# The written key of each head pair turned through DRAM and VectorE's blocks, and the outputs' transposes moved behind the joined visit

## The chip, the cores and the metric

One core of a Trainium2 chip runs the kernel in one launch. The engines are TensorE (PE: matmuls and transposes; its weight loads are listed apart as PEld), VectorE (DVE), ScalarE (ACT), GpSimd (POOL) and SyncE (SP); SP and ACT also issue the DMAs, each in its own order. The metric is device time in microseconds, the median of several runs of the same program.

## The reference

One layer of a hybrid decoder over 512 positions and 2,048 channels, in fp32, then a final RMSNorm. What matters here is the first half of the channels: 16 heads of 64 channels with a gated delta-rule recurrence.

```
z = rms_norm(x) @ W_in           # r, k, v, two small inputs, gate | pool input, pool gate
w = exp(-exp(-softplus(-(w0 + tanh(wd) @ Wup)) - 0.5));  a = sigmoid(a0 + ad @ Aup)
kk = normalised(k * k_k);  k = k * (1 + (a - 1) * k_a)
S_t = S_{t-1} * w_t - (S_{t-1} kk_t)(kk_t a_t)^T + v_t k_t^T;   y_t = S_t r_t
y = group_norm(y) + (r . k . r_k) v;  times silu(gate)
pool branch: trailing means over 2/4/8/16 positions, a map per group, times silu(gate)
x = x + concat(y, pool) @ W_out;  x = x + sigmoid(x @ W_pg + b) * (p @ W_ple)
```

## The kernel before

Every large product is made of three matmuls of split operands (a high part and a rest), on tiles of 128 channels by 512 positions. The input is normalised and transposed once (`hhi`, `hlo`). The recurrence then runs in eight rounds of two heads (j = 0 to 7, 128 channels each), in chunks of 64 positions (8 a round). Within a round the chunk-by-chunk state update is a chain of small matmuls with short DVE and ACT steps between them. Between these the kernel issues pieces of a long stream of large matmuls (`pump(n)` issues n of them): the projections of the next rounds and of the pool branch (tiles zk, zr, zv, zg, zb). In this part PE's instructions keep the order of the program; the other engines' orders are set by a scheduler with priorities. Behind the rounds come the projection with W_out (acc_o) and the gate's with W_pg (acc_g).

The weights come by `wsplit`: SP issues the load of 256 KB into `raw` (four buffers), ACT makes the high part (L132, four buffers), DVE the rest (L133). SP's queue goes in order, and a load waits there until its buffer is free.

The steps of a round, as the change touches them:

- `prepare(j)` (DVE, L591 to L601, then a split) makes the written key `bk`: for each chunk, 128 columns with the two products that are written into the state (line 596 one half, line 600 the other), with channels on partitions.
- `scores(j)` multiplies `bk` by the read side `ar` (matmuls pm), masks the result into `mt` and sends a part of it to DRAM (`nd`, four writes) and back (`n`, two reads into 32x32 systems). It runs inside the previous round's `recur`, behind that round's first chunk.
- `invert(j)`: 31 short DVE steps (tm, xw) that invert the 32x32 triangles, two steps at each hand-over of the previous round's recurrence; the result goes through DRAM (`xd`) to `x1`.
- `gather(j)`: transposes v (pv) and the written key (pbk) on PE, with ACT copies out of PSUM: `bkn` is the key with positions on partitions. Here stand also the next round's decay and key norms, and the previous round's output (`pending.pop()()`, below). Then the joined visit: y1 = block transposes of x1 on DVE (L723), matmuls pq, pmv, px, and copies on ACT that complete x1 (L745).
- `recur(j)`: per chunk py and the add zs on DVE (the first hand-over of the chunk), pu and its copy uv on ACT, ps (with `bkn`) and the state's update sbd on DVE. Behind the eighth chunk come the outputs' statistics and their normalisation (`ysb`, L842 to L851).
- `finish`, kept in `pending` by `recur(j-1)` and called in `gather(j)`: transposes `ysb` (pyt, 4 transposes), scales it on ACT (yo), two products on DVE (L861, L862), and a store to DRAM that ACT issues (L863).

Of the kernel before, what the change touches and what calls it, by code (L numbers as in the profile page):

```python
# [9 lines left out]
F32 = mybir.dt.float32  # L10
# [3 lines left out]
ALU = mybir.AluOpType  # L14

P = 128
T = 512
# [4 lines left out]
NJ = DR // P  # L22
LORA = 64
C = 64
NCH = T // C
# [9 lines left out]
def trunk_kernel(ctx: ExitStack, tc: tile.TileContext, x, p, norm_g, w_in, mu, w0, w_up, a0, a_up,  # L35
                 k_k, k_a, r_k, ln_w, ln_b, w_pool, pool_scale, w_out, w_ple, w_pg, b_pg, final_g, out):
    nc = tc.nc
# [122 lines left out]
    def tr(*a):  # L160
        i = nc.tensor.transpose(*a)
        return tc.keep_in_program_order(i) if pin[0] else i
# [414 lines left out]
    def prepare(j):  # L577
        k_, r_, v_ = need("k", j), need("r", j), need("v", j)
        pw, ipw, tha = pws.pop(j)
        kk = kks.pop(j)  # L580
        if j + 1 < NJ:
            load_ab(j + 1)


        ar = rw.tile([P, NCH // 2, 4, C], F32, name=f"ar{j}", tag="ar", bufs=2)
        bk = rw.tile([P, NCH // 2, 4, C], F32, name=f"bk{j}", tag="bk")
        k4 = kk.rearrange("p (q c t) -> p q c t", c=2, t=C)
        pw4 = pw.rearrange("p (q c) t -> p q c t", c=2)
# [11 lines left out]
        nc.vector.tensor_tensor(bk[:, :, 1:3, :], k4, i4, ALU.mult)  # L600
        nc.vector.scalar_tensor_tensor(kp, r_, dp(49, j), kp, ALU.mult, ALU.mult)  # L601
        kph = rw.tile([P, T], F32R, name=f"kph{j}", tag="t", bufs=4)
        kpl = rw.tile([P, T], F32R, name=f"kpl{j}", tag="t", bufs=4)
        split(kph, kpl, kp)

        st_[j] = dict(pw=pw, ar=ar, bk=bk, v_=v_, kp=(kph, kpl))

    def scores(j):
        ar, bk, v_ = (st_[j][n_] for n_ in ("ar", "bk", "v_"))
        kph, kpl = st_[j].pop("kp")  # L610

        mt = rw.tile([P, 2, 8, 2, C], F32, name=f"mt{j}", tag="mt", bufs=2)
# [13 lines left out]


        ps = psM.tile([P, T], F32, name=f"pbo{j}", tag="m")
        mm(ps, blk, kph, start=True, stop=False)
        mm(ps, blk, kpl, start=False, stop=True)  # L630
        bv = rw.tile([P, T], F32, name=f"bv{j}", tag="bv", bufs=2)
        nc.vector.tensor_tensor(bv, ps, v_, ALU.mult)

        nd = dram.tile([2, 2, 8, 32, 32], F32, name=f"nd{j}", tag="nd")
        for par in range(2):
            pb = 64 * (1 - par)
            for b in range(2):
                rows = slice(pb + 32 * b, pb + 32 * b + 32)
                nc.sync.dma_start(out=nd[par, b].rearrange("u r c -> r u c"),
                                  in_=mt[rows, par, :, 1 - par, 32 * b:32 * b + 32])  # L640
        nb = []
        for i in range(2):
            t_ = rw.tile([P, 16, 32], F32, name=f"n32{j}_{i}", tag=("kk", "kp")[i])
            nc.sync.dma_start(out=t_, in_=nd[:, :, :, 16 * i:16 * i + 16, :].rearrange(
                "a b u r c -> (a b u) r c").unsqueeze(0).to_broadcast([4, 32, 16, 32]))
            nb.append(t_)
        st_[j].update(mt=mt, nb=nb, bv=bv)


    def invert(j):  # L650
# [26 lines left out]

    def gather(j):
        d = st_[j]
        bk, v_, mt = d.pop("bk"), d.pop("v_"), d["mt"]  # L680
        if j + 1 < NJ:
            prepare_key(j + 1)
            decay_and_rate(j + 1)
# [7 lines left out]
        nc.scalar.copy(uv[64:128, 1::2, :], pv[64:128])  # L691


        bkn = rw.tile([P, NCH, P], F32, name=f"bkn{j}", tag="bkn")
        for hf in range(2):
            ps = psM.tile([P, T], F32, name=f"pbk{j}_{hf}", tag="m")
            for i in range(4):
                ch = 4 * hf + i
                tr(ps[:, i * P:(i + 1) * P], bk[:, ch // 2, 2 * (ch % 2):2 * (ch % 2) + 2, :], ident)
            nc.scalar.copy(bkn[:, 4 * hf:4 * hf + 4, :], ps.rearrange("p (c n) -> p c n", n=P))  # L700

        pump(H4)

        d.update(uv=uv, bkn=bkn)
        if j + 1 < NJ:
            norm_key(j + 1)
        pump(H5)
        if pending:
            pending.pop()()
        pump(HX)  # L710

        x1 = d["x1"]
# [6 lines left out]
        y1 = rw.tile([P, 8, 32], F32, name=f"y1{j}", tag="tm")  # L719

        with tc.issue_after(late[0].ins):
            for pb in (0, 64):
                yt = nc.vector.transpose(y1[pb:pb + 32], x1[pb:pb + 32, :, 0:32])  # L723
# [23 lines left out]
        nc.scalar.copy(zsp[0][64:128, :].rearrange("p (h t) -> p h t", h=2), psv[64:128, 0:2, :])  # L747
        nc.scalar.copy(mv.rearrange("p q (h t) -> p (q h) t", h=2), psv)
        d["mv"] = mv
        pump(2 * H1)  # L750


    def recur(j, work, between):
        d = st_.pop(j)
        pw, ar, mt, bv, uv, bkn, mv, x1 = (d[n_] for n_ in ("pw", "ar", "mt", "bv", "uv", "bkn", "mv", "x1"))
        hop = [0]
        HC1, HC2, HC3 = HC
        lead = [None]
# [12 lines left out]
        for ch in range(NCH):  # L771
# [8 lines left out]
            if ch > 0:  # L780
# [67 lines left out]
        nt8 = rw.tile([P, 8, 1], F32, name=f"nt8{j}", tag="nt8")  # L848
        rsqrt(rs8, ve8, nt8)
        for i in range(8):  # L850
            nc.vector.tensor_scalar(y8[:, i, :], y8[:, i, :], mvr[:, i, 0:1], rs8[:, i, :],  # L851
                                    ALU.subtract, ALU.mult)

        def finish():
            sg = need("g", j)
# [11 lines left out]
    HC, HT, HX = (6, 9, 9), 130, 13  # L867
    HS, HN = 5, 2
    HP = 1000
    pending = []  # L870
    need("k", 0)
    need("r", 0)
    prepare_key(0)
# [304 lines left out]
```

## Time and profile before

| | us |
|---|---|
| median of 3 runs (1093.36 to 1094.28) | 1093.37 |
| the profiled execution | 1094.06 |
| its span, first to last instruction | 1092.3 |
| PE busy | 1067.4 |
| DVE busy | 707.9 |
| ACT busy | 448.2 |
| POOL busy | 74.4 |
| ACT copies out of pbk, 16 | 8.8 |

The granted TensorE clock is 0.998 of full. The rounds lie between about 110 and 727 us of the span, one about every 75 us. Rows of the timeline read: start, length, engine, line, operation, written tile <- read tiles, shape, count, and in brackets how long the engine had idled before it and what ended that. A matmul's length there is its latency: matmuls overlap, and the time that one takes of PE is the distance between starts. Rows of groups end with the busy time, the mean of one in ns, and the idle time before them. Rows of windows give, for a stretch, the busy time (and count) of PE, PEld, DVE, ACT and POOL, then the granted clock, the DMA engines' busy share and GB/s.

### The profile page before, as it was taken

Reading aid. Unit: us, or ns where it says so; the run is one execution under the profiler, and the core shown is the slowest. Engines: PE = TensorE matmul, PEld = TensorE weight load, DVE = VectorE, ACT = ScalarE, POOL = GpSimd, SP = SyncE. Lnnn points to the kernel's source line nnn. Section 1 sums busy time; section 2 is a strip of 40 time slices with the busy share of each in tenths; the row PEclk is TensorE's granted clock in tenths of the full one; section 3 lists DMA queues with packets and bytes.
Section 4 is the critical chain, followed back from the end, with each engine's and each line's share of the span. In section 5 each row is a group of like instructions: output and inputs, shape, how many; then the busy total and the mean of one; then the engine's idle time right before and its main releaser. Section 6 shows DMA issues by size and latency. Waiting matters only on the chain.

```text
span 1092.3 us, 17194 instructions
## 1 busy us (share of the span) xinstructions
PE 1067.4 (98%) x6060; PEld 879.1 (80%) x6060; DVE 707.9 (65%) x1835; ACT 448.2 (41%) x917; POOL 74.4 (7%) x180
## 2 busy tenths in 40 slices
PE   5999999999999999999999999999999999999996
PEld 4888878888888888787888788888888888888885
DVE  6687867878779679678886956454433424445366
ACT  7633534435335335353443344544222222233337
POOL 2100010110110110100101101000000000000000
PEclk9999999999999999999999999999999999999999
DMA  7433433332423333333334242774534438454534
GB/s 233 116 97 97 112 92 79 102 101 72 127 81 102 105 91 89 95 83 90 94 93 120 79 138 94 231 242 163 171 123 141 164 97 261 129 187 147 174 105 154
DMA packets 178485, 138.56 MB, mean 127 GB/s; under 512 B 34677, under 2 KB 139742, under 8 KB 178398
## 3 DMA queue, kind: packets, MB, share of 16 engines
q1 hardware_dynamic: 157694, 103.89, 32.2%
q10 hardware_dynamic: 20704, 33.56, 9.5%
q8 instruction: 48, 0.79, 0.3%
q14 instruction: 39, 0.32, 0.1%
HBM read 118.02 MB, written 18.87 MB: 125 GB/s over the span
## 4 chain that ended last, share of the span: by engine, by line
PE 88%; DVE 5%; DMA 3%; ACT 2%; issue 1%; SPq 0%; ACTq 0%; DVEq 0%
PE acc_o L157 16%; PE acc_g L157 16%; PE zb L157 15%; PE zv L157 8%; PE zr L157 7%; PE zg L157 7%; PE zk L157 6%; DMA n<-nd 2%; PE py L157 2%; PE pple L157 2%; PE pu L157 2%; PE pm L157 1%; PE pp L157 1%; PE ps L157 1%; PE pmv L157 1%
## 5 line engine op out<-in xcount | busy, mean ns | idle before, releaser
L133 DVE TENSOR_TENSOR wlo_g<-raw_g,whi_g 128x512 fp32r<-128x512 f32 x84 | 56.9, 683 | 78.7 <-ACT whi_g L132 78.5
L157 PE MATMUL zb<-hhi,whi_b 128*128 128x512 f32 x256 | 106.3, 415 | 0.0
L133 DVE TENSOR_TENSOR wlo_o<-raw_o,whi_o 128x512 fp32r<-128x512 f32 x64 | 43.9, 690 | 92.3 <-ACT whi_o L132 92.2
L157 PE MATMUL zb<-hhi,wlo_b 128*128 128x512 f32 x256 | 100.5, 393 | 0.0
L157 PE MATMUL acc_o<-whi_o,ylo 128*128 128x512 f32 x256 | 100.2, 391 | 0.0
L157 PE MATMUL acc_o<-whi_o,yhi 128*128 128x512 f32 x256 | 99.9, 390 | 0.0
L157 PE MATMUL zb<-hlo,whi_b 128*128 128x512 f32 x256 | 99.8, 390 | 0.0
L157 PE MATMUL acc_o<-wlo_o,yhi 128*128 128x512 f32 x256 | 99.7, 389 | 0.0
L132 ACT CAST whi_g<-raw_g 128x512 fp32r<-128x512 f32 x84 | 51.9, 620 | 105.5 <-PE acc_g L157 60.3
L157 PE MATMUL acc_g<-whi_g,x2hi 128*128 128x512 f32 x208 | 81.2, 391 | 0.0
L157 PE MATMUL acc_g<-wlo_g,x2hi 128*128 128x512 f32 x208 | 81.0, 389 | 0.0
L157 PE MATMUL acc_g<-whi_g,x2lo 128*128 128x512 f32 x208 | 80.6, 389 | 0.0
L132 ACT CAST whi_o<-raw_o 128x512 fp32r<-128x512 f32 x64 | 39.9, 623 | 97.8 <-PE acc_o L157 97.8
L813 POOL TENSOR_SCALAR s0p<-sbd,pw 64x64 f32<-64x64 f32 x96 | 56.7, 590 | 338.5 <-DVE sbd L806 253.7
L132 ACT CAST whi_b<-raw_b 128x512 fp32r<-128x512 f32 x64 | 39.7, 620 | 87.1 <-PE zv L157 34.9
L133 DVE TENSOR_TENSOR wlo_b<-raw_b,whi_b 128x512 fp32r<-128x512 f32 x64 | 43.7, 684 | 34.2 <-ACT whi_b L132 33.0
L157 PEld LDWEIGHTS zb<-hhi,wlo_b 128*128 128x128 f32 x256 | 48.0, 188 | 11.0
L661 DVE TENSOR_TENSOR xw<-xw,tm 128x60 f32<-128x60 f32 (+24 forms) x248 | 51.9, 209 | 6.8
L157 PEld LDWEIGHTS acc_o<-wlo_o,yhi 128*128 128x128 f32 x256 | 48.1, 188 | 10.0
L157 PEld LDWEIGHTS acc_o<-whi_o,ylo 128*128 128x128 f32 x256 | 48.1, 188 | 9.9
L157 PEld LDWEIGHTS acc_o<-whi_o,yhi 128*128 128x128 f32 x256 | 48.1, 188 | 9.6
L157 PEld LDWEIGHTS zb<-hhi,whi_b 128*128 128x128 f32 x256 | 48.3, 189 | 8.4
(285 smaller groups left out, 2546.8 us busy)
## 6 DMA issues: line engine op xcount, KB each, us to landing
raw_b<-in_w_in_dram SPq DMA_DIRECT2D x64, 256.0 KB
raw_o<-in_w_out_dram SPq DMA_DIRECT2D x64, 256.0 KB
raw_g<-in_w_pg_dram SPq DMA_DIRECT2D x64, 256.0 KB
raw_k<-in_w_in_dram SPq DMA_DIRECT2D x32, 256.0 KB
raw_r<-in_w_in_dram SPq DMA_DIRECT2D x32, 256.0 KB
raw_v<-in_w_in_dram SPq DMA_DIRECT2D x32, 256.0 KB
raw_g<-in_w_in_dram SPq DMA_DIRECT2D x32, 256.0 KB
n<-nd SPq DMA_DIRECT2D x16, 256.0 KB
```

Of the source, the lines that this page charges most:

```text
L132: nc.scalar.copy(hi, raw)
L133: nc.vector.tensor_tensor(lo, raw, hi.bitcast(F32), ALU.subtract)
L157: i = nc.tensor.matmul(*a, **k)
L661: nc.vector.tensor_tensor(xw[:, 0:n_, s + 1:32], xw[:, 0:n_, s + 1:32], tm[:, 0:n_, 0:w_], ALU.add)
L813: nc.gpsimd.tensor_scalar(s0p[hc, :], nxt[hc, hc], pcn[hc], None, ALU.mult)
```

## The change

The written key is no longer transposed by PE. `prepare` writes `bk` to DRAM as it is (`bkd`, one DMA on SP of 128 rows of 4 KB). `scores`, behind the issue of n, issues four reads on SP that bring it back with its 32x32 blocks at their new places (`bg`, in bk's own buffer): each fills 32 partitions, in runs of 32 numbers. `turn_key` then turns each block in place with two DVE block transposes of 128x512, into one lasting `bkn`. The first round's turn stands in `gather(0)`; every other in the previous round's last chunk, issued behind the zs of that chunk. Moreover `finish` is called behind the joined visit and half of the stream's piece that follows it, where it stood ahead of the visit; and the scaling of the next key (reciprocal) is tied behind both block transposes of x1 and the last normalisation of the outputs.

```diff
         split(kph, kpl, kp)
 
-        st_[j] = dict(pw=pw, ar=ar, bk=bk, v_=v_, kp=(kph, kpl))
+        bkd = dram.tile([P, NCH * P], F32, name=f"bkd{j}", tag="bkd")
+        nc.sync.dma_start(out=bkd, in_=bk.rearrange("p q s c -> p (q s c)"))
+        st_[j] = dict(pw=pw, ar=ar, bk=bk, bkd=bkd, v_=v_, kp=(kph, kpl))
+
+    bkn = rw.tile([P, NCH, P], F32, name="bkn")
+
+    def turn_key(j, hf):
+        cs = slice(4 * hf, 4 * hf + 4)
+        nc.vector.transpose(bkn[:, cs, :].rearrange("p c (b k) -> p (c b) k", k=32),
+                            st_[j]["bg"][:, cs, :, :].rearrange("p c b k -> p (c b) k"))
...
-            nc.sync.dma_start(out=t_, in_=nd[:, :, :, 16 * i:16 * i + 16, :].rearrange(
+            n_ = nc.sync.dma_start(out=t_, in_=nd[:, :, :, 16 * i:16 * i + 16, :].rearrange(
                 "a b u r c -> (a b u) r c").unsqueeze(0).to_broadcast([4, 32, 16, 32]))
             nb.append(t_)
-        st_[j].update(mt=mt, nb=nb, bv=bv)
+        bg = rw.tile([P, NCH, 4, 32], F32, name=f"bg{j}", tag="bk")
+        with tc.issue_after(n_.ins):
+            for q in range(4):
+                nc.sync.dma_start(out=bg[32 * q:32 * q + 32],
+                                  in_=st_[j]["bkd"].rearrange("(b k) (c q i) -> q k c b i", b=4, q=4, i=32)[q])
+        st_[j].update(mt=mt, nb=nb, bv=bv, bg=bg)
...
-        bkn = rw.tile([P, NCH, P], F32, name=f"bkn{j}", tag="bkn")
-        for hf in range(2):
-            ps = psM.tile([P, T], F32, name=f"pbk{j}_{hf}", tag="m")
-            for i in range(4):
-                ch = 4 * hf + i
-                tr(ps[:, i * P:(i + 1) * P], bk[:, ch // 2, 2 * (ch % 2):2 * (ch % 2) + 2, :], ident)
-            nc.scalar.copy(bkn[:, 4 * hf:4 * hf + 4, :], ps.rearrange("p (c n) -> p c n", n=P))
-
+        if j == 0:
+            turn_key(0, 0)
+            turn_key(0, 1)
         pump(H4)
...
         pump(H5)
-        if pending:
-            pending.pop()()
         pump(HX)
...
         if j + 1 < NJ:
-            with tc.issue_after(yt.ins):
+            with tc.issue_after(yt[0].ins), tc.issue_after(yt[1].ins), tc.issue_after((normed or yt)[-1].ins):
                 scale_key(j + 1)
...
-        pump(2 * H1)
+        pump(H1)
+        if pending:
+            pending.pop()()
+        pump(H1)
...
+            if ch == NCH - 1 and j + 1 < NJ:
+                with tc.issue_after(lead[0].ins):
+                    turn_key(j + 1, 0)
+                    turn_key(j + 1, 1)
             psu = psS.tile([P, T], F32, name=f"pu{j}_{ch}", tag="s")
```

PE in `gather(2)`, before (pa is a decay product, pv and pbk are the transposes of v and of the written key, zb a pool projection of the stream):

```order
L157 MATMUL pa_3348<-lal,uaz_571 128x512
L161 MATMUL pv_3354<-ident,sv_2448 128x128 x4
L161 MATMUL pbk_0_3362<-ident,bk_2604 128x128 x4
L161 MATMUL pbk_1_3368<-ident,bk_2604 128x128 x4
L157 MATMUL zb_3377<-hhi,whi_b_0_1812 128x512
L157 MATMUL zb_3377<-hlo,whi_b_0_1812 128x512
```

Now:

```order
L157 MATMUL pa_3350<-lal,uaz_571 128x512
L161 MATMUL pv_3356<-ident,sv_2441 128x128 x4
L157 MATMUL zb_3366<-hhi,whi_b_0_1816 128x512
L157 MATMUL zb_3366<-hlo,whi_b_0_1816 128x512
L157 MATMUL zb_3366<-hhi,wlo_b_0_1817 128x512
```

The two groups of pbk are gone and the stream's matmul follows pv; over the whole program PE's order differs in nothing else but the place of pyt.

DVE in the last chunk of `recur(1)`, before (zs is the chunk's hand-over, tm and xw the last inversion step, wlo the weights' low parts, BN_STATS the outputs' statistics):

```order
L784 TENSOR_TENSOR zs_569<-py_4_2980,mv_2568 64x128
L133 TENSOR_TENSOR wlo_b_1_1842<-raw_b_1_1839,whi_b_1_1841 128x512
L657 TENSOR_TENSOR tm_2820<-xw_2819,n_1_2730 128x8
L661 TENSOR_TENSOR xw_2819<-xw_2819,tm_2820 128x8
L133 TENSOR_TENSOR wlo_b_2_1848<-raw_b_2_1845,whi_b_2_1847 128x512
L842 BN_STATS st_3283<-ysb_2619 128x6 x4
```

Now:

```order
L793 TENSOR_TENSOR zs_569<-py_4_2980,mv_2551 64x128
L133 TENSOR_TENSOR wlo_b_1_1846<-raw_b_1_1843,whi_b_1_1845 128x512
L671 TENSOR_TENSOR tm_2820<-xw_2819,n_1_2725 128x8
L614 STREAM_TRANSPOSE bkn<-bg_2727 128x512
L675 TENSOR_TENSOR xw_2819<-xw_2819,tm_2820 128x8
L614 STREAM_TRANSPOSE bkn<-bg_2727 128x512
L133 TENSOR_TENSOR wlo_b_2_1852<-raw_b_2_1849,whi_b_2_1851 128x512
L855 BN_STATS st_3285<-ysb_2614 128x6 x4
```

The two block transposes of the written key stand between zs and the statistics, one of them ahead of the last inversion step.

ACT in `gather(5)` and at the start of `recur(5)`, before (x is x1's second half, L863 the store of the previous round's output, uv the first chunk's copy):

```order
L735 COPY q_6027<-pq_6010 32x256 x2
L747 COPY zs_568<-pmv_6030 64x128
L748 COPY mv_6066<-pmv_6030 128x512
L863 DMA yd<-yo_5985 128x512
L132 CAST whi_k_1_3408<-raw_k_1_3406 128x512
L137 CAST dh_5286<-u_5961 128x512
L745 COPY x_5807<-px_6047 32x8x32 x2
L794 COPY uv_5921<-pu_0_6107 64x64 x2
```

Now:

```order
L741 COPY q_5994<-pq_5977 32x256 x2
L753 COPY zs_568<-pmv_5997 64x128
L754 COPY mv_6033<-pmv_5997 128x512
L751 COPY x_5795<-px_6014 32x8x32 x2
L132 CAST whi_k_1_3397<-raw_k_1_3395 128x512
L137 CAST dh_5257<-u_5938 128x512
L874 ACTIVATE yo_6047<-pyt_6042,dprm 128x512
L807 COPY uv_5911<-pu_0_6086 64x64 x2
L132 CAST whi_k_2_3403<-raw_k_2_3401 128x512
L877 DMA yd<-yo_6047 128x512
```

The copies of x1 stand directly behind mv, and the output's scaling and store behind them, the store behind the first chunk's copy.

More of the change, by code (lines that the diff above doesn't have):

```diff
@@ L679, in gather @@
         d = st_[j]
-        bk, v_, mt = d.pop("bk"), d.pop("v_"), d["mt"]
+        v_, mt = d.pop("v_"), d["mt"]
         if j + 1 < NJ:
@@ L691, in gather @@
         nc.scalar.copy(uv[64:128, 1::2, :], pv[64:128])
-        bkn = rw.tile([P, NCH, P], F32, name=f"bkn{j}", tag="bkn")
-        for hf in range(2):
-            ps = psM.tile([P, T], F32, name=f"pbk{j}_{hf}", tag="m")
-            for i in range(4):
-                ch = 4 * hf + i
-                tr(ps[:, i * P:(i + 1) * P], bk[:, ch // 2, 2 * (ch % 2):2 * (ch % 2) + 2, :], ident)
-            nc.scalar.copy(bkn[:, 4 * hf:4 * hf + 4, :], ps.rearrange("p (c n) -> p c n", n=P))
+        if j == 0:
+            turn_key(0, 0)
+            turn_key(0, 1)
         pump(H4)
-        d.update(uv=uv, bkn=bkn)
+        d.update(uv=uv)
         if j + 1 < NJ:
@@ L721, in gather @@
         with tc.issue_after(late[0].ins):
-            for pb in (0, 64):
-                yt = nc.vector.transpose(y1[pb:pb + 32], x1[pb:pb + 32, :, 0:32])
+            yt = [nc.vector.transpose(y1[pb:pb + 32], x1[pb:pb + 32, :, 0:32]) for pb in (0, 64)]
         if j + 1 < NJ:
-            with tc.issue_after(yt.ins):
+            with tc.issue_after(yt[0].ins), tc.issue_after(yt[1].ins), tc.issue_after((normed or yt)[-1].ins):
                 scale_key(j + 1)
@@ L749, in gather @@
         d["mv"] = mv
-        pump(2 * H1)
+        pump(H1)
+        if pending:
+            pending.pop()()
+        pump(H1)
     def recur(j, work, between):
         d = st_.pop(j)
-        pw, ar, mt, bv, uv, bkn, mv, x1 = (d[n_] for n_ in ("pw", "ar", "mt", "bv", "uv", "bkn", "mv", "x1"))
+        pw, ar, mt, bv, uv, mv, x1 = (d[n_] for n_ in ("pw", "ar", "mt", "bv", "uv", "mv", "x1"))
         hop = [0]
@@ L850, in recur @@
         for i in range(8):
-            nc.vector.tensor_scalar(y8[:, i, :], y8[:, i, :], mvr[:, i, 0:1], rs8[:, i, :],
-                                    ALU.subtract, ALU.mult)
+            last = nc.vector.tensor_scalar(y8[:, i, :], y8[:, i, :], mvr[:, i, 0:1], rs8[:, i, :],
+                                           ALU.subtract, ALU.mult)
+        normed.append(last)
         def finish():
@@ L869, in trunk_kernel @@
     HP = 1000
-    pending = []
+    pending, normed = [], []
     need("k", 0)
```

## The prediction

> **What bounds the kernel now.** I read the busy shares first, then the chain of work that ended last, then the stages.
>
> ```profile
> PE 1067.4 (98%) x6060; PEld 879.1 (80%) x6060; DVE 707.9 (65%) x1835; ACT 448.2 (41%) x917; POOL 74.4 (7%) x180
> PE 88%; DVE 5%; DMA 3%; ACT 2%; issue 1%; SPq 0%; ACTq 0%; DVEq 0%
> 409.00:484.00 75.00, 74.17 (x487) 60.47 (x486) 60.06 (x184) 32.53 (x72) 8.72 (x15) 1.00 0.34 93
> 727.00:900.00 173.00, 173.00 (x787) 143.13 (x787) 65.33 (x99) 50.82 (x86) 0.00 (x0) 1.00 0.45 149
> ```
>
> PE is the bound: 98% of the span, 88% of the chain. The third row is one 75 us round of the recurrence part (about 110 to 727 us): PE 74.17 busy, DVE 60.06 (80%), ACT 32.5. Behind it (fourth row) PE has no gap at all, so a microsecond saved in the rounds is not given back later. What matters is then PE's own issue time in the rounds, and the few places where PE waits there. The list of PE's waits has two causes in the rounds that come more than once or cost 1 us:
>
> ```profile
> PE py L157 <- DVE sbd L806: 1.9, 6, 0.6
> PE pu L157 <- ACT x L745: 1.0, 1, 1.0
> ```
>
> So PE is nearly free of waits on average, and yet DVE at 80% has stretches where it is full. Those decide how much of a PE saving arrives.
>
> **What the change removes: the key's transposes.** Each round issues 8 transposes (pbk) to PE. Their cost is the time by which they push back the next matmul, read from PE's timeline:
>
> ```profile
> 184.87 0.60 PE L161 MATMUL pv<-ident,sv 128*128 128x128 f32 x4
> 185.30 1.04 PE L161 MATMUL pbk<-ident,bk 128*128 128x128 f32 x8
> 186.10 0.47 PE L157 MATMUL zv<-hhi,whi_v 128*128 128x512 f32 x1
> ...
> 259.26 1.28 PE L161 MATMUL pbk<-ident,bk 128*128 128x128 f32 x8
> 260.30 0.48 PE L157 MATMUL zb<-hhi,whi_b 128*128 128x512 f32 x1
> ...
> 558.57 1.19 PE L161 MATMUL pbk<-ident,bk 128*128 128x128 f32 x8
> 559.68 0.50 PE L157 MATMUL pp<-dh,whi_wp 128*128 128x512 f32 x1
> ...
> PEld pbk L161 <- ACT sig L532: 0.4, 2, 0.3
> ```
>
> The eight start at 185.30 and the next matmul at 186.10: 0.80 us, 0.10 each. Six of the eight rounds look like this; the other two take 1.04 and 1.11 us, because the tile had to wait for its PSUM buffer (the last row, from the list of waits: two waits for ACT's sig). Without the transposes the next matmul needs no such buffer, so all of it goes: 6 x 0.80 + 1.04 + 1.11 = **6.95 us**.
>
> ```profile
> L161 PE MATMUL pbk<-ident,bk 128*128 128x128 f32 x64 | 8.7, 274 | 0.0
> L700 ACT COPY bkn<-pbk 128x512 f32<-128x512 f32 x16 | 8.8, 589 | 0.2
> L723 DVE STREAM_TRANSPOSE y<-x 32x256 f32<-32x256 f32 x16 | 6.9, 430 | 1.2 <-DMA x<-xd 1.0
> L600 DVE TENSOR_TENSOR bk<-kk,ipw 128x512 f32<-128x512 f32 x8 | 5.5, 686 | 0.0
> ```
>
> The 274 ns of the first row are the latency of one transpose, not its share of PE. The Trainium skill's "TensorE: Matmul & The Clock Gate" (Part 4: PE-mode transpose) gives about 275 ns for one in a kernel; by that as a price 64 x 0.275 = 17.6 us would go and the time would be near 1077, which the timeline's 0.80 us for eight excludes.
>
> ACT loses 16 copies, 9.4 us, off the path.
>
> **What it adds on DVE.** Sixteen block transposes of 128x512, two a round. No such size is in the trace. The same operation on 256 columns takes 430 ns, another operation on 512 columns 686. Below: 0.43 (as if free of size); above: 2 x 0.43 = 0.86. I take 0.70, nearest to the row of the same width: 1.4 us a round. From the second round on they stand behind the recurrence's last hand-over (zs of the eighth chunk), where DVE has time:
>
> ```profile
> 251.51 0.28 DVE L784 TENSOR_TENSOR zs<-py,mv 64x128 f32<-64x128 f32 x1 [0.74 <-PE py L157]
> 254.93 0.69 DVE L133 TENSOR_TENSOR wlo_b<-raw_b,whi_b 128x512 fp32r<-128x512 f32 x1 [2.24 <-ACT whi_b L132]
> 256.64 0.61 DVE L842 BATCH_NORM_STATS2 st<-ysb 128x6 f32<-128x64 f32 x4 [1.01 <-ACT ysb L827]
> ```
>
> After zs it idles 2.24 and then 1.01 us for casts and copies that PE's own pace releases. 1.4 us fit, so I cost the turns at nothing; without this cover they cost up to 1.4 us a round. Queued behind them on DVE are the last inversion step (its result goes through DRAM to x1), the weights' low parts and the statistics. The first round's turn has no such gap; there the scores are far off:
>
> ```profile
> 126.22 0.68 DVE L600 TENSOR_TENSOR bk<-kk,ipw 128x512 f32<-128x512 f32 x1
> 132.82 1.30 PEld L157 LDWEIGHTS pm<-ar,bk 64*128 64x128 f32 x22 [0.35 <-issue]
> ...
> 204.27 0.68 DVE L600 TENSOR_TENSOR bk<-kk,ipw 128x512 f32<-128x512 f32 x1
> 207.71 2.06 PE L157 MATMUL pm<-ar,bk 64*128 64x128 f32 x32
> ```
>
> The key is done 5.9 us before the scores (132.82 - 126.90) in that round, and 2.8 us in the next.
>
> What is late next is x1 -> y1 -> the joined visit (pq). The tightest visit:
>
> ```profile
> 341.92 0.89 DVE L723 STREAM_TRANSPOSE y<-x 32x256 f32<-32x256 f32 x2
> 344.55 0.63 PE L157 MATMUL pq<-y,mt 32*32 32x32 f32 x28
> ```
>
> y1 ends 1.74 us before pq. PE now arrives there without the output's 4 transposes (0.43 by pv's rows), so about 1.3 us are left: nothing lost.
>
> **What it adds on the queues.** Per round one write of 512 KB and four reads of 128 KB, in runs of 32 numbers (128 bytes): 1,024 packets each. The nearest row is the four nd writes, which are 32 KB each in 128-byte runs:
>
> ```profile
> 436.50:438.50 2.00, 1.92 (x10) 1.27 (x9) 1.75 (x4) 0.88 (x3) 0.00 (x0) 1.00 0.41 66
> 435.70 1.99 SPq L639 DMA_DIRECT2D nd<-mt  x4
> 439.05 1.15 SPq L644 DMA_DIRECT2D n<-nd  x2
> 476.18 0.27 DVE L784 TENSOR_TENSOR zs<-py,mv 64x128 f32<-64x128 f32 x1
> 105.35 4.76 PE zv L157 x21
> ```
>
> 1,024 packets took 0.41 of the engines for 2.00 us. One read therefore takes between 0.82 (engines only) and 2.0 us (at that issue pace), the four 3.3 to 8 us; the write, as many bytes in longer runs (4 KB), no longer than they. The reads queue on SP between weight loads; the first also waits for the write's landing and for the scores to be done with bk, both over by the time n has been issued. Behind it on SP stand the weights. They have cover: four raw and four split buffers ahead of PE, each 12 matmuls of 0.227 us (last row: 21 in 4.76), 2.7 us, together near 22 us. The reads start behind n (issued at 439 to 440) and the turn comes behind the zs of 476, some 35 us later. I take zero.
>
> **What it moves.** The output's 4 transposes, their ACT pass, two DVE products and the store's issue on ACT's queue go from ahead of the joined visit to behind it. PE's cost is the same. On ACT this mends one wait:
>
> ```profile
> 496.85 0.68 DVE L862 TENSOR_TENSOR yo<-yo,sg 128x512 f32<-128x512 f32 x1
> 497.56 0.33 ACTq L863 DMA_DIRECT2D yd<-yo  x1
> 499.42 0.73 ACT L745 COPY x<-px 32x256 f32<-32x256 f32 x2
> 500.20 0.49 PE L157 MATMUL pu<-zs,x 128*128 128x128 f32 x2 [1.02 <-ACT x L745]
> ```
>
> The store's issue sat in ACT's queue until DVE had finished yo at 497.53, and the copies of x1 behind it came at 499.42; PE stood for 1.02 us. Now they stand ahead of the output's pass, so **1.0 us** goes. The store now holds up casts further on that are not due.
>
> **What is given back.** In two rounds (the scores of the sixth and the seventh pair) DVE is full from the statistics to the key's second product (bk), and the scores wait for that:
>
> ```profile
> 407.30:431.70 24.40, 24.40 (x204) 20.20 (x202) 24.01 (x62) 14.18 (x30) 2.09 (x3) 1.00 0.31 86
> 481.20:506.60 25.40, 24.38 (x202) 20.00 (x201) 24.91 (x63) 14.78 (x31) 1.71 (x3) 1.00 0.29 79
> 431.91 1.86 PEld L157 LDWEIGHTS pm<-ar,bk 64*128 64x128 f32 x32 [0.35 <-DVE bk L600]
> 507.02 0.64 PEld L157 LDWEIGHTS pm<-ar,bk 64*128 64x128 f32 x10 [0.35 <-DVE bk L600]
> ```
>
> DVE is 98% busy for 25 us, and the list of work between the two points is not shorter after the change (61 and 62 instructions before, 62 and 62 now). PE will come 0.8 us earlier in the first, and 0.8 + 1.0 in the second (it has lost the x1 wait too), and must wait it out: 0.8 + 1.8 = **2.6 us** back. The other rounds have 2.8 us and more between bk and the scores, like the two above.
>
> **Sum:** 6.95 + 1.0 - 2.6 = 5.35 us. The profiled execution (1094.06) would become 1088.7; it lies 0.69 above the median of the runs, so the median goes from 1093.37 to **1088.0**.
>
> **Rivals.**
> 1. *All of it arrives.* DVE's list may run a little faster in the full stretches (a split of weights more on one side of bk is 0.69 us), and then 6.95 + 1.0 = 7.95 us go: 1085.4. For it: PE's wait at bk was only 0.35 us. Against: DVE is at 98% there.
> 2. *DVE takes most back.* The waits py <- sbd (1.9 us now) and the scores' grow in all seven rounds by about 0.8 us, the amount by which PE is ahead, so 5.6 of the 7.95 go: 1091.0, hardly to be told from no change. For it: DVE at 80% in the whole part. Against: those 2.8 us and more.
> 3. *Slower: the turns land on the path.* If the casts' waits are no cover, because what follows on DVE is late by all of 1.4 us through to y1 or bk, the eight rounds cost 11.2 and return 7.95: 1096.6. It decides from about 1.0 us a round uncovered. Against it: 3.2 us of idle time in the row above.
> 4. *Slower: the strided reads hold the queue.* If a read ran on one DMA engine instead of 16, four would take 16 x 3.3 = 52 us, 30 beyond the weights' cover, in each of eight rounds: 1325. At four engines (13 us) nothing shows; it decides from 22 us a round. The nd row speaks against it. The Trainium skill's "VectorE: DVE Perf Modes" (The three transpose paths; Rules for kernel authors) speaks against this change: it calls a plain DMA with transposing strides a trap and wants a 128x128 transpose on TensorE. Here the strided side keeps whole 128-byte runs and the turn inside the blocks is DVE's, so I give it little.
>
> That the transposes do not go is excluded: in PE's order the pbk rows are missing and nothing else but the output's transposes has moved.
>
> **How the numbers follow.** Chances: forecast 0.57 (own range 1086 to 1090), rival 1 0.20, rival 2 0.13, rival 3 0.07, rival 4 0.03. The range for 8 in 10 runs from a microsecond below rival 1 to a microsecond beyond rival 2: 1084.3 to 1092.0. A measurement of this kernel tells 0.2%, 2.2 us, from no change. Faster by more: forecast, rival 1 and a little of rival 2 (1091.0 lies just below the 1091.2 that counts), 0.80. Within: the rest of rival 2 and the shallow end of rival 3, 0.12. Slower: 0.08.
>
> **What would show it.** Right: no pbk rows on PE, PE's count 64 lower; pv followed at once by a matmul of 512 columns; two 128x512 block transposes of 0.6 to 0.8 us a round where DVE idled; no PE wait on ACT's x; PE's waits on bk at two scores of 1 to 2 us. Wrong: a DVE wait for the read block at the turn, casts that wait for raw weights in the rounds, a PE wait at pq, or block transposes well above 0.86 us.

## The result

The changed kernel takes 1086.24 us (median, 1085.56 to 1088.76) against 1093.68 us (1093.1 to 1094.64) for the kernel before in the same session: ratio 0.9934, 95% interval 0.9922 to 0.9947. That is 7.4 us less, where 5.35 were forecast; a second session gave the same ratio (0.9934, 0.9922 to 0.9946).

### The profile page after: what moved, and what is told of

Same layout as the page of the kernel before. It is cut to its first block, busy times and chain, and to the rows that moved or that the text cites. A ratio compares the mean times of both kernels' runs of the same rounds, so it can differ in the third digit from the quotient of the medians.

```text
span 1084.8 us, 17101 instructions
## 1 busy us (share of the span) xinstructions
PE 1058.8 (98%) x5996; PEld 873.2 (80%) x5996; DVE 716.5 (66%) x1851; ACT 441.0 (41%) x901; POOL 76.1 (7%) x180
## 4 chain that ended last, share of the span: by engine, by line
PE 88%; DVE 6%; DMA 2%; ACT 2%; issue 1%; SPq 0%; ACTq 0%; DVEq 0%
PE acc_o L157 16%; PE acc_g L157 16%; PE zb L157 14%; PE zv L157 8%; PE zk L157 7%; PE zr L157 7%; PE zg L157 6%; PE py L157 2%; PE pple L157 2%; PE pu L157 1%; PE pm L157 1%; DMA n<-nd 1%; PE pp L157 1%; PE ps L157 1%; PE pmv L157 1%
```

## The profile after

The busy line of the changed kernel's page (busy us, share of the span, instructions):

```profile
PE 1058.8 (98%) x5996; PEld 873.2 (80%) x5996; DVE 716.5 (66%) x1851; ACT 441.0 (41%) x901; POOL 76.1 (7%) x180
```

PE's list of waits in it (tile, line, who released it: us in all, times, longest):

```profile
PE pm L157 <- DVE bk L600: 2.9, 2, 1.6
PE py L157 <- DVE sbd L819: 1.7, 6, 0.4
PE pu L157 <- DVE zs L793: 0.4, 1, 0.4
```

PE has 64 instructions less and is still busy for 98%. The wait for ScalarE's x is gone; a new one stands at the scores, twice, as forecast.

PE's timeline of the changed kernel, in the round whose transposes the prediction showed first, and at the two scores (start, us, engine, line):

```profile
183.31 0.60 PE L161 MATMUL pv<-ident,sv 128*128 128x128 f32 x4
183.66 0.47 PE L157 MATMUL zv<-hhi,whi_v 128*128 128x512 f32 x1
...
427.14 1.05 PE L157 MATMUL pm<-ar,bk 64*128 64x128 f32 x14 [1.37 <-DVE bk L600]
...
501.04 1.16 PE L157 MATMUL pm<-ar,bk 64*128 64x128 f32 x16 [1.56 <-DVE bk L600]
```

From pv's first transpose to the next 512-column matmul it is 0.35 us now and was 1.23 (184.87 to 186.10). The group of the block transposes (count, busy us, mean ns of one, idle us before them):

```profile
L614 DVE STREAM_TRANSPOSE bkn<-bg 128x512 f32<-128x512 f32 x16 | 10.9, 696 | 0.0
```

They take 0.696 us and have no idle time before them: they never wait for their read.

Matching the instructions of PE in the two traces one by one, and adding up how the distance from each to the next has changed, gives 7.54 us for the two profiled executions: transposes of the key -7.55, the waits for x -1.14, the scores +3.07, the outputs' transposes -2.60 at their old place and +2.48 at the new one, the recurrence's products py and pu -2.05, the rest (start of the program, small steps) +0.25. "Ledger" means this sum in what follows. It compares one execution with one execution, and two executions of one kernel can differ by some microseconds; where the profiled one lies far from its kernel's median, the text says so.

## The experiments

All ratios are to the kernel before, run beside the experiment. The first two take the change apart.

**The key alone.** The outputs' pass is put back.

```diff
         pump(H5)
+        if pending:
+            pending.pop()()
         pump(HX)
...
-        pump(H1)
-        if pending:
-            pending.pop()()
-        pump(H1)
+        pump(2 * H1)
```

> The change without its second part: the key goes through DRAM and VectorE as in the changed kernel, but the outputs' pass stands where it stood before, ahead of the joined visit. My theory: the key alone takes 7.5 us off PE (the ledger of the two traces) and gives about 3 us back at two scores; the wait of PE for ScalarE's x in one round (1.0 us) is back, but in that round it only takes the place of part of the 1.56 us wait at the scores behind it. So 1086.2 to 1087.5, ratio to the kernel before 0.9932 to 0.9945, PE's list of waits with ACT x at 1.0 us and the wait at bk about 1 us smaller. Rival (the move matters by itself, because the waits for zs in the recurrence that went with it were due to the outputs' products on VectorE): 1088 to 1089.5, ratio 0.995 to 0.9965.

1092.76 against 1095.04, ratio 0.9973 (0.9959 to 0.9987). My expectation fell, and the value lies above the rival's range too, though the interval reaches into it: only 40% of the gain is there. The profiled execution (1089.7) is the fastest of ten, 3.1 us below the median, so the ledger below shows where time is lost rather than all of it. PE's list of waits in this run:

```profile
PE px L157 <- issue: 1.5, 2, 0.9
PE pyt L161 <- DVE ysb L863: 1.3, 2, 0.7
PE pm L157 <- DVE bk L600: 1.1, 2, 0.6
```

Its PE timeline at one of the outputs' transposes:

```profile
337.41 0.62 PE L161 MATMUL pyt<-ident,ysb 128*128 128x128 f32 x2
338.75 0.77 PE L161 MATMUL pyt<-ident,ysb 128*128 128x128 f32 x2 [0.72 <-DVE ysb L863]
339.28 0.48 PE L157 MATMUL zb<-hhi,whi_b 128*128 128x512 f32 x1
```

And its ScalarE timeline at one of the two waits at px, whose operand q ScalarE copies:

```profile
194.16 0.35 ACTq L876 DMA_DIRECT2D yd<-yo  x1
194.68 0.74 ACT L743 COPY q<-pq 32x256 f32<-32x256 f32 x2 [3.17 <-DVE yo L875]
```

At their old place the outputs' transposes (pyt) meet VectorE while it normalises the rows they read, and ScalarE's copy of q stands, at this place, behind the store's issue, which waits for VectorE's yo. In the kernel before the transposes just fitted (VectorE's timeline, then PE's):

```profile
338.93 1.87 DVE L851 TENSOR_SCALAR ysb<-ysb,mvr,rs 128x64 f32<-128x64 f32 x8
```
```profile
340.50 0.69 PE L161 MATMUL pyt<-ident,ysb 128*128 128x128 f32 x4
340.94 0.48 PE L157 MATMUL zb<-hhi,whi_b 128*128 128x512 f32 x1
```

The last row was normalised at 340.80, while the four were being issued. With the key's transposes gone PE is there 0.9 us earlier (counted from pv), and the four take 1.87 us from the first to the next matmul (337.41 to 339.28) instead of 0.44. By the ledger pyt takes 6.12 us in seven rounds here, 2.48 in the changed kernel; px costs 1.68 more than there, the scores 1.83 less. So the two parts are no sum: the moved pass is what lets the key's saving through.

**The move alone,** on the kernel before: the same two places, edited the other way.

> The kernel before with nothing but the second part: the outputs' pass moved behind the joined visit, the key still turned by TensorE. My theory: PE's wait for ScalarE's x (1.02 us) goes, and in that round PE comes 1.0 us earlier to the scores, where VectorE is full, so most of it comes back there: 0 to 1.0 us less than the kernel before, ratio 0.999 to 1.000. Rival (the recurrence's waits for zs, about 2 us of the whole gain that I had not predicted, belong to the move): 2 to 3 us less, ratio 0.997 to 0.998.

Ratio 0.9994 (0.9981 to 1.0007): nothing to be told from no change, as the theory had it. The ledger has the waits for x gone and 1.09 us back at the scores; py takes 1.96 us more in this execution, which lies 1.5 us above its kernel's median. Key alone 3.0 us, move alone 0.7 us, both 7.2 us at these ratios: about half of the gain needs both (each of the three is known to about 1.5 us).

**The key alone, store on another queue.** Was the store on ScalarE's queue the trouble?

```diff
-            nc.scalar.dma_start(out=yd[j], in_=yo)
+            nc.sync.dma_start(out=yd[j], in_=yo)
```

> The key's part alone (as in the run of that name, outputs ahead of the joined visit), but the outputs' store is issued on SyncE's queue and not on ScalarE's. It tells apart the two things that ate the saving there: PE's waits at px (0.68 and 0.86 us, ScalarE's copy of q stood behind the store's issue, which waited for VectorE's yo) and PE's waits at the outputs' transposes for VectorE's normalised rows (0.12 to 0.84 us in five rounds). My reading: the px waits go, 1.5 us, of which 0.9 comes back at the scores of the seventh pair; the transposes' waits stay. So 0.6 to 1.0 us below the key's part alone, still 2 us and more above the changed kernel. Rival (the store's place on the queue is all that the move was for): it comes down to the changed kernel's time.

Ratio 0.9970 (0.9960 to 0.9981), no better than the key alone. One of the two px waits went, the other stayed at 0.86 us. ScalarE there, in this run:

```profile
488.90 0.62 ACT L132 CAST whi_k<-raw_k 128x512 fp32r<-128x512 f32 x1 [0.21 <-PE zg L157]
492.33 0.62 ACT L137 CAST dh<-u 128x512 fp32r<-128x512 f32 x1 [2.81 <-DVE u L421]
492.96 0.74 ACT L743 COPY q<-pq 32x256 f32<-32x256 f32 x2
```

No store stands in the queue, but a cast that waits for VectorE's u does, and VectorE has no idle time ahead of u (none from 484.73 to the end of u at 492.30). The transposes pyt take as long as with the key alone (6.11 us). So the move's effect is not the store's place on a queue: it takes the outputs' VectorE work and what depends on it out of the stretch ahead of the visit.

**No turn at all.** Write, reads and block transposes are left out, and the turned key is set to zero once, so the part of the computation that adds the key's products to the state is left out; its matmuls still run.

```diff
-        nc.sync.dma_start(out=bkd, in_=bk.rearrange("p q s c -> p (q s c)"))
...
-                nc.sync.dma_start(out=bg[32 * q:32 * q + 32],
...
-                    turn_key(j + 1, 0)
-                    turn_key(j + 1, 1)
+    nc.gpsimd.memset(bkn, 0.0)
```

> The changed kernel without the key's way: no write, no reads, no block transposes; the turned key is zero throughout, so the part of the computation that adds it to the state is left out (the matmuls on it still run). My theory: the way costs nothing, being covered by idle time of VectorE and by weights loaded ahead, so the time is that of the changed kernel, 1085.3 to 1086.5, and the two waits at the scores are still there. Rival a (the turns cost VectorE time that returns at the full stretches): the two waits shrink by up to 1.4 us each, so 1083.4 to 1084.5. Rival b (the reads slow the weights' loads or VectorE's writes): 1 to 4 us less, spread over all rounds, with shorter DMA times in the recurrence part.

Ratio 0.9942 (0.9927 to 0.9957), which includes the changed kernel's 0.9934 and lies, if anything, above it. The waits at the scores are still 3.0 us. The way through DRAM and VectorE costs nothing that can be measured, and neither rival holds.

**Every turn twice.**

```diff
-                    turn_key(j + 1, 0)
-                    turn_key(j + 1, 1)
+                    for _ in range(2):
+                        turn_key(j + 1, 0)
+                        turn_key(j + 1, 1)
```

> The changed kernel with each block transpose at the last chunk done twice (14 pairs of 128x512 turn a second time): VectorE has 2 x 0.70 = 1.4 us more in each of seven rounds. My theory: VectorE still idles 1.9 to 2.4 us between the last hand-over and the next round's key in the changed kernel, and that takes it: 0 to +1.5 us over the changed kernel (1086.2 to 1087.7), with most of what does appear in the two full rounds' waits at the scores. Rival (turns land on the path, my third of the prediction): +1.4 us in each of seven rounds, 1096.

Ratio 0.9935 (0.9919 to 0.9950). Another 1.4 us of VectorE a round costs nothing that can be measured either: 1096 is excluded, the cover behind the last zs is real and not used up.

**Every read twice.** Four more strided reads a round, into a scratch in DRAM.

```diff
+            bg2 = dram.tile([P, NCH, 4, 32], F32, name=f"bx{j}", tag="bx")
+            for q in range(4):
+                nc.sync.dma_start(out=bg2[32 * q:32 * q + 32], in_=...)
```

> The changed kernel with the four strided reads of each round issued a second time, into a scratch in DRAM: 32 more transfers of 1,024 packets of 128 bytes, behind the first ones on SyncE's queue. My theory (the reads are hidden, there are some 20 us of weights ahead): within 1 us of the changed kernel, ratio to it 0.999 to 1.001, no cast that waits for raw weights in the rounds. Rival (the reads hold the queue or the DMA engines, my fourth of the prediction in a milder form): one set of reads costs as much as this second one, so the excess over the changed kernel is what the change itself pays: 2 us or more, with casts or PE waiting for raw weights, or a longer trip of n.

1097.59 us, ratio 1.0023 (1.0012 to 1.0033): about 10 us lost over the changed kernel, ten times what my theory allowed. The profile shows where: not in eight rounds but for the most part in the first. SyncE's queue there:

```profile
103.85 3.11 SPq L663 DMA_DIRECT2D bx<-bkd  x4
107.06 2.94 SPq L129 DMA_DIRECT2D raw_b<-in_w_in_dram  x2
110.09 2.55 SPq L683 DMA_DIRECT2D xd<-xw  x4
112.74 0.55 SPq L129 DMA_DIRECT2D raw_b<-in_w_in_dram  x1
113.38 7.72 SPq L129 DMA_DIRECT2D raw_g<-in_w_in_dram  x2
121.27 1.88 SPq L690 DMA_DIRECT2D x<-xd  x4
```

In the changed kernel, and then from this run's list of SyncE's own waits (the longest of these, 6.8 us, is the one here):

```profile
113.83 1.82 SPq L686 DMA_DIRECT2D x<-xd  x4
115.75 6.18 SPq L129 DMA_DIRECT2D raw_g<-in_w_in_dram  x3
```
```profile
SPq L129 <- DVE wlo_b L133: 49.0, 20, 6.8
```

PE's timeline behind it:

```profile
124.59 1.43 PE L157 MATMUL pq<-y,mt 32*32 32x32 f32 x32 [4.68 <-DVE y L733]
125.94 1.97 PE L157 MATMUL pmv<-uv,mt 64*64 64x64 f32 x32
...
128.84 0.80 PE L157 MATMUL zb<-hhi,whi_b 128*128 128x512 f32 x1
```

And stretches of that run (length; busy us of PE, PEld, DVE, ACT, POOL; granted clock; DMA share, GB/s):

```profile
119.90:124.60 4.70, 0.02 (x2) 0.04 (x2) 3.23 (x7) 1.71 (x3) 0.00 (x0) 0.81 0.47 106
124.60:127.00 2.40, 2.31 (x52) 2.11 (x54) 2.40 (x2) 0.73 (x2) 0.00 (x0) 0.50 0.71 209
131.00:133.00 2.00, 2.00 (x6) 1.52 (x6) 1.73 (x3) 0.00 (x0) 0.00 (x0) 0.50 0.11 27
133.00:135.00 2.00, 2.00 (x11) 1.68 (x10) 0.00 (x0) 0.88 (x3) 0.00 (x0) 0.98 0.98 362
```

SyncE's order has changed with the extra reads: two loads of raw_g, which stand behind the reads of x1 in the changed kernel, stand ahead of them here and take 7.7 us, 6.8 of it a wait until VectorE has read the buffer (wlo_b). x1 comes late, PE stands for 4.68 us, and its granted clock is 0.50 until 133: pmv takes 1.97 us here, 1.15 in the changed kernel (at 120.85). By the ledger this one place costs 8.6 us, 4.7 of it the wait and 3.9 the slow clock. From 135 us on, with the remaining 28 extra reads, this run is 2.8 us longer than the changed kernel's first profile and 1.1 longer than its second, and two executions of the changed kernel differ by 1.9; against the second all of the 1.1 lies before 170 us. So no cost of the reads shows in the later rounds, and the loss in the first is the place of x1's reads in SyncE's queue, which the scheduler sets; why it set it so was not tested. In the changed kernel x<-xd is issued at 113.83 and PE does not wait. The rival's number has come, its reading has not: what a second set of reads costs is not what the first one costs, since the kernel without any is no faster.

**The two full rounds relieved.** VectorE is full up to bk in two rounds; here it has less to do before it.

```diff
-        nc.vector.tensor_scalar(sig, sig, 0.5, 0.5, ALU.mult, ALU.add)
+        nc.scalar.activation(sig, sig, AF.Identity, scale=0.5, bias=half_)
...
-        nc.vector.tensor_scalar(tha, tha, 0.5, 0.5, ALU.mult, ALU.add)
+        nc.scalar.activation(tha, tha, AF.Identity, scale=0.5, bias=half_)
...
+        with tc.issue_after(b2.ins):
             nc.vector.scalar_tensor_tensor(kp, r_, dp(49, j), kp, ALU.mult, ALU.mult)
```

> The changed kernel with VectorE relieved ahead of the key's second product: the two affine steps behind the tanh (tha and sig, 0.42 us each) go to ScalarE, and the bonus product (0.74 us) is put behind bk. My theory (in the rounds of the sixth and the seventh pair VectorE is full up to bk and PE waits 1.37 and 1.56 us for it): bk comes 1.5 us and more earlier there, both waits go down to 0 to 0.4 us, and 2 to 3 us are gained over the changed kernel, ratio to the kernel before 0.9905 to 0.9918. Rival (PE that is earlier there only waits longer at the next place, the first state product of the recurrence behind the DRAM trip of n, because that trip starts at the scores): the waits at bk go, those for sbd grow by as much, and nothing is gained.

Ratio 0.9932 (0.9916 to 0.9948): no gain. The waits at bk did fall, from 2.9 to 0.8 us, but PE's wait for sbd is 6.0 in this profile. The profiled execution (1091.43) is the slowest of six, 4.3 us above the median, so this 6.0 is not what the kernel usually pays. PE's list in it, then VectorE's:

```profile
PE py L157 <- DVE sbd L822: 6.0, 6, 1.7
PE pm L157 <- DVE bk L602: 0.8, 2, 0.5
PE pbo L157 <- DVE kpl L138: 0.3, 1, 0.3
```
```profile
DVE tm L674 <- DMA n<-nd: 22.5, 8, 3.9
```

The profile looks as the rival has it, with two causes that this run does not separate: what was put behind bk makes kpl and the last mt later (by 0.7 us in the two rounds), and the DRAM trip of n, which starts at mt, took longer in this execution.

**The changed kernel again.**

> The changed kernel once more, as the measure for the runs beside it. Ratio to the kernel before 0.993 as in its first runs. In the profile: PE's first wait for the state (sbd) of a round is not a matter of this kernel but of how long the DRAM trip of the scores' diagonal (nd, then n) took in that execution: the sums from the last mt to the first product of the inversion were 71.7 us over eight rounds in the profile where py waited 1.7 us, 74.8 and 76.1 us in the two where it waited 3.2 and 3.6 us. So I expect the sum and the wait to go together again, by about 0.3 to 0.5 us of wait per us of trip.

The ratio was the same, 0.9934. VectorE's wait for n and PE's wait for sbd, from the lists of waits of the changed kernel's first profile, of this one, and of the run without a turn:

```profile
DVE tm L671 <- DMA n<-nd: 15.7, 8, 4.0
PE py L157 <- DVE sbd L819: 1.7, 6, 0.4
```
```profile
DVE tm L671 <- DMA n<-nd: 18.3, 8, 4.6
PE py L157 <- DVE sbd L819: 3.0, 7, 0.8
```
```profile
DVE tm L665 <- DMA n<-nd: 19.8, 8, 4.2
PE py L157 <- DVE sbd L806: 3.6, 6, 1.2
```

The page says that PE waits for VectorE's sbd; what VectorE itself waits for is a DMA. The inversion's first step (tm) needs n and stands in VectorE's queue ahead of the next sbd. VectorE in the changed kernel's second round:

```profile
219.12 0.19 DVE L671 TENSOR_TENSOR tm<-i,n 128x31 f32<-128x31 f32 x1 [1.29 <-DMA n<-nd]
...
222.00 0.59 DVE L819 SCALAR_TENSOR_TENSOR sbd<-ps,pw,s0p 64x64 f32<-64x64 f32 x2
```

One kernel differs by 1.3 us in PE's wait between two executions, and on the whole longer waits for n come with longer waits at py (17.0 and 1.2, 19.0 and 3.2, 20.9 and 3.8 in the runs with the key alone, the turns twice and the move alone), though not strictly: 18.3 and 1.9 in the kernel before, 18.2 and 3.4 in the run with the store on another queue. Whether the step holds sbd up is what the next run tests.

**The inversion two hops later,** so that its first step stands behind that sbd. A hop is a place at a hand-over of the recurrence where the program issues inversion steps: HS hops are let pass first, then HN steps are issued at each.

```diff
-    HS, HN = 5, 2
+    HS, HN = 7, 2
```

> The changed kernel with the inversion's first step two hops later on VectorE, behind the hand-over (sbd) of the third chunk instead of ahead of it; two steps a hop as before. In the changed kernel VectorE stands at that first step until the DRAM trip of n has landed (the trip from n's issue to the step took 6.1 to 8.4 us over the runs), the hand-over behind it is late, and PE waits for it 1.7 to 3.1 us in all. My theory: that wait goes, the spread from run to run with it. The inversion now ends two hops later, at the last chunk, and x1 comes later for the joined visit, where y1 had 0.14 to 2.6 us to spare: if the two hops come back there the visit waits, some 2 to 4 us a round in seven rounds. I expect the second: 1095 to 1110, PE waits at pq for y in the rounds, none for sbd in the fourth chunk.

1085.18 against 1094.91, ratio 0.9907 (0.9891 to 0.9922). I had expected it slower. The mechanism was right and the size wrong: the wait for sbd goes (3.13 us less at py by the ledger against the changed kernel's first profile, and VectorE waits for n once instead of eight times), waits at pq come in three rounds, but of 2.8 us in all and not of 2 to 4 a round (3.76 at pq by the ledger), and since PE then comes later to the scores, 1.68 us of the waits there go too. That adds up to about 1 us; the profile is 1.7 us shorter, the rest of it in the program's start, which the edit does not touch. PE's list:

```profile
PE pq L157 <- DVE y L729: 2.8, 3, 1.1
PE pm L157 <- DVE bk L600: 1.2, 2, 0.7
PE py L157 <- DVE sbd L819: 0.3, 1, 0.3
```

**The same with three steps in every hop** (HS, HN = 7, 3), **with that and VectorE relieved ahead of bk, and with a third step in four hops only** (`HN + (hop[0] in (10, 13, 16, 19))`).

> As the run with the later start, but three inversion steps a hop, so that the inversion ends as early as in the changed kernel or earlier. Theory (the wait for sbd is only the place of that step in VectorE's queue): the wait for sbd behind the DRAM trip goes, no wait at pq, 1 to 2.5 us under the changed kernel, ratio to the kernel before 0.991 to 0.9925. Rival (VectorE is so full from there on that three steps a hop hold up the hand-overs zs and sbd of the later chunks, 0.45 us each hop): the waits for zs and sbd in the chunks from the fourth to the seventh grow by as much, 0.993 or more.

> The later start with three steps a hop, and VectorE relieved ahead of the key's second product (two affine steps on ScalarE, the bonus product behind bk). If what was gained at the scores in that run came back at the DRAM trip (my reading of it), it should now arrive: about 2 us less than the later start with three steps a hop alone, ratio to the kernel before 0.989 to 0.991. If the gain was never there (VectorE's list behind bk only got longer by what was put there: pbo waits for kpl 0.7 us, mt ends 0.66 us later after the scores), the two runs are within 0.1% of each other.

> As the run with the later start (first inversion step behind the third chunk's hand-over), with a third step in four hops, those between zs and sbd of the fourth to the seventh chunk, where VectorE idled for PE (0.45 and 1.14 us in one chunk of that run); in the hops between sbd and zs it stays at two. The inversion so ends one hop earlier. Theory: PE's waits at pq (1.13, 0.73 and 0.93 us in three rounds of that run) mostly go, but about 1.7 us of what goes in two of these rounds comes back at the scores, where VectorE is full; no new waits at zs (which three steps in every hop brought, 2.06 us). So 1 to 2 us below the later start with two steps, ratio to the kernel before 0.989 to 0.9905. Rival: the hand-overs of the state wait behind the third step, and it is no better, 0.9905 to 0.992.

Ratios 0.9921 (0.9907 to 0.9934), 0.9920 (0.9907 to 0.9933) and 0.9908 (0.9892 to 0.9925). The first lies in my theory's range, but with the rival's waits: three steps everywhere remove the wait at pq, but those for zs grow (+2.06 us by the ledger at pu, against the changed kernel) and 1.2 us of the waits for sbd are left. The relief ahead of bk again gives nothing: VectorE waits for n only once here (4.0 us, in the first round), so its gain was not lost at the trip, and my reading of the earlier run was wrong. Against its own partner, the run with three steps alone, it took 1.90 us off the scores and lost 0.70 at pbo, 0.21 at pu and 0.7 in small steps: 0.3 us net. The mixed one does what was expected in its profile, PE's list:

```profile
PE pm L157 <- DVE bk L600: 2.9, 2, 1.5
PE pu L157 <- DVE zs L793: 0.8, 2, 0.4
```

No wait at pq, none worth listing at py, and the scores' back at 2.9. Against the changed kernel's first profile the ledger has 3.05 us less, nearly all of it at py (-3.34). Its ratio is in the rival's range and not in mine, and it is that of the later start with two steps; which of the two is better cannot be told. Both are below the changed kernel's 0.9934 (0.9922 to 0.9947), with intervals that touch or slightly overlap its own: by the ratios they are 2.8 to 3.0 us faster than the changed kernel, which they were not run beside, and the best versions of this study.

## Why the prediction came out

**The key's transposes, 6.95 us: 7.55.** The mechanism and the place were right. I took the time from the first pbk to the next matmul (0.80 a round); the step from pv to what follows it also shrank, from 0.43 to 0.35, which is the 0.6 us that was missing.

**The wait for x, 1.0 us: 1.14, but not by itself.** The row was right (it is gone), the reading of it was thin. I named the store in ScalarE's queue as the cause; but behind the store, in the same queue, a cast waited for VectorE's u before the copies of x came at 499.42:

```profile
498.89 0.62 ACT L137 CAST dh<-u 128x512 fp32r<-128x512 f32 x1 [0.35 <-DVE u L421]
```

With the key alone and the store elsewhere such a cast still held up q. And I wrote of the move that "PE's cost is the same" and gave it 1.0 us, all of which my own working gives back at the scores of that round (0.8 + 1.0): by my terms the move was worth nothing and the key alone the whole 5.35. Alone the move is indeed worth nothing measurable, but the key alone brought 3.0, and with the key the move is worth 0.9973 - 0.9934, 4 us. The step that failed is that sum of two independent terms. The two rows that would have shown it stood in the trace of before: VectorE's normalised rows end at 340.80, the transposes that read them start at 340.50. They have no slack, and a saving of PE ahead of them is lost there unless they move; so it came out in four of the seven rounds of the run with the key alone.

**Given back at the scores, 2.6 us: 3.07.** Right in place and cause; by the ledger 1.44 and 1.63 us where I had 0.8 and 1.8, and the waits are now 1.37 and 1.56 us. That rival 1 (1085.4) lies nearer to the time is chance: its mechanism, a shorter list on VectorE, is excluded by these waits, which grew.

**Turns and queues at nothing.** Right: leaving them out gains nothing, doubling the turns costs nothing measurable, a turn takes 0.696 us where I took 0.70. My reason for the queues, 22 us of weights ahead, looked at the weights alone and left out that x1's reads stand in the same queue. Doubling the reads found that, and rival 4 in a form I had not thought of: not one read on a slow path, but one transfer's place behind weights that wait for their buffers. The Trainium skill's "VectorE: DVE Perf Modes" (The three transpose paths), cited with rival 4, warns of DMAs with transposing strides; no run here bears that out for a side that keeps 128-byte runs, since leaving the reads out gains nothing.

**The visit, "about 1.3 us are left".** Too much. The tightest visit of the changed kernel, VectorE's timeline and PE's:

```profile
486.46 0.42 DVE L729 STREAM_TRANSPOSE y<-x 32x256 f32<-32x256 f32 x1
```
```profile
487.02 0.69 PE L157 MATMUL pq<-y,mt 32*32 32x32 f32 x32
```

0.14 us are left. I took only the output's transposes off PE's way to the visit, but the key's stand ahead of it too: from the first pv to the first pq it was 10.53 us in that round and is 9.17, so by my rows 1.74 - 0.43 - 0.80, about 0.5, should have been left at the visit I showed (0.94 were). And in the round of the rows above y1 ends later, 9.03 us behind pv instead of 6.95; I had looked only at the visit that was tightest before. Nothing was lost, but by less than I thought; with the inversion two hops later it is the visit that waits.

**What was not forecast** is the 2.05 us less at the recurrence's products. Two executions of the changed kernel differ by 1.7 us there, so most of it may belong to the two executions and not to the change; the medians, which differ by as much as the profiles do, speak for a part of it being real. Against the one profile of the kernel before, pu (without the wait for x) is 0.7 to 1.3 us less in every profile with the inversion's start unchanged, the key alone and the move alone among them, while py lies between 1.3 us less and 4.2 more. That stays open. It is what put the time at 1086.2 and not at 1088.

Rivals 2 and 3 fell. Rival 2 needs 5.6 us given back at py and the scores of all rounds: 3.07 came back, at two scores, and the waits at py are 1.7 and 3.0 us in the two profiles of the changed kernel, 1.9 before. Rival 3 fell because the turns are not on the path.

## What to carry to other kernels

Before adding up the parts of a change, look at each place that the saved engine reaches earlier and read how much its operand has to spare there (340.80 against 340.50): a move that is worth nothing alone can be what lets a saving arrive. When PE waits for a VectorE result, read what VectorE itself waited for just before; an in-order queue hides a DMA behind the name of an arithmetic instruction. And test "hidden" by doubling as well as by leaving out: leaving out showed a cost of zero, doubling showed one place where a transfer's position in the queue cost 8.6 us.

## What the hardware showed beyond what was expected

In one wait of 4.68 us PE's granted clock fell to 0.50: it was 1.00 before and has a mean of 0.81 over the 4.70 us, which puts the fall about 2.9 us into them. It stayed at 0.50 for some 8 us more (124.6 to 133), though PE was busy nearly all that time, and 3.9 us were lost on top of the wait. The Trainium skill's "TensorE: Matmul & The Clock Gate" (Part 1: The HAM clock gate) states half rate after an idle window of about 3.4 us, and full rate after about as long a busy one. The first half agrees with this trace roughly (2.9 us of idling by that estimate, in a wait longer than 3.4); the way back took 8 us from PE's first instruction (the 32x32 and 64x64 matmuls of the visit), or 4.2 us from the first 512-column matmul at 128.84. The waits of 1.37 and 1.56 us at the scores left the granted clock at 1.00.

The trip of a small block through DRAM and back (nd, then n) varied by 2.7 us between rounds and executions: from n's issue to the first use it was between 5.7 and 8.4 us over the runs in which that use stood ahead of sbd in VectorE's queue.
